# Row maxima of an attention kernel from 64-row products taken in pairs

## The chip, the cores and the metric

The kernel runs on one core of a Trainium2 chip. The metric is the device time of one execution in microseconds (us). Five engines of the core run their own instruction streams beside each other: TensorE (products; PE in the profile, its weight loads PEld), VectorE (DVE), ScalarE (ACT), GpSimd (POOL) and SyncE (SP, which issues DMA transfers). Products are written to PSUM, which has 8 banks of 128 x 512 float32 values.

## The reference

Two layers work on 1024 latent tokens (width 1024, a 16 x 64 grid) and 256 context tokens; the output is the latent stream after a last norm. Layer 0 has global attention (8 query heads, 2 key heads, all 1280 keys) beside banded attention (8 heads, 2 key heads, the 256 context keys and a band of 128 tokens to each side, with a learned sink logit per head). Layer 1 has a convolution branch beside attention over a 2-D neighbourhood (8 heads, 8 rows x 16 columns and the context keys, with a table of biases). Head width is 64.

```python
s = einsum("bqhgd,bkhd->bhgqk", q, k) * ATTN_SCALE      # 64 ** -0.5
s = s + bias                                            # band mask or bias table
p = softmax(concatenate([s, sink_col]))[..., :-1]       # sink in the banded heads only
out = einsum("bhgqk,bkhd->bqhgd", p, v)
```

All is float32. A softmax does not change when one number is subtracted from a whole row; the kernel subtracts the row's maximum, and a value near it does as well.

## The kernel before

**Numbers.** A float32 operand is held as two float32r values, a high part (the rounded value) and a low part (the rest), so that one accurate product becomes two or three fast ones. `split` (L323) makes both parts, the high one on ScalarE and the low one on GpSimd or VectorE. Projections are three products each (`mm3`, L346 to L349: high x high, high x low, low x high).

**Attention tiles.** Head width is 64 and the array has 128 rows, so a product of 128 rows holds two 64-row halves. For a group of 512 queries (four heads of 128 queries in layer 0, 512 queries of one head in layer 1):
- `QH`: the high part of Q in rows 0 to 63 and again in rows 64 to 127.
- `QL`: the low part of Q in rows 0 to 63, and above it in rows 64 to 67 minus the row maxima (rows 68 to 75 hold the two parts of the sink's term in the banded heads).
- `KA`: the high part of K in rows 0 to 63, its low part in rows 64 to 127.
- `KB`: the high part of K again in rows 0 to 63 (`copy_k`, L592, a ScalarE copy), ones in rows 64 to 67 (`k_tiles`, L381, for layer 1 and `kv_tiles`, L575, for layer 0).

A tile of scores is then two products into one bank: `KA` x `QH` (L503, 128 rows) and `KB` x `QL` (L507, 68 rows), the second of which subtracts the maxima too. ScalarE takes the exponential (L515), `split` makes both parts of the result, and `flush` (L435) multiplies with V in three products (L445 to L447, of which L446 has 64 output columns) that also sum the denominators. In the banded heads one further product per group (L450, 76 rows) adds the sink's part to the denominators.

**Row maxima.** They must be there before the first score tile of a group. `attn_prep` (L392) does this for a group: load Q, products of `QH` with `KA` into banks of the tag `mx` (`maxes`, L608 in layer 0, L1416 in layer 1), reductions on VectorE straight from the bank (L616, L627, L635, L1426, L1435), one small reduction over pieces, a transpose (L415), and a product with a mask (L416) that writes minus the maxima into `QL`. There are 40 groups in layer 0 (4 units of heads, each 10 query blocks, two of them with context keys alone) and 16 in layer 1. Per group there are:
- layer 0, all groups: four products of 256 context keys, two to a bank;
- layer 0, global heads, 8 of 10 blocks: eight products of 512 keys, one to a bank;
- layer 0, banded heads, 8 of 10 blocks: four products of 384 keys (256 at the ends);
- layer 1: four products of 256 keys, two to a bank, and four of 320 or 440 keys.

Every bank is filled and then reduced, and the tag `mx` has two banks, so that one can be filled while the other is reduced.

**Order of the work.** `attn_gen` (L428) yields after each step, and `weave` (L533) runs a fixed number of its steps against steps of a second generator with projection work (the next unit's projections, gates, output products). `prepare` (L473) runs a few steps of the preparations of groups further on in each step of the current group; a preparation is opened two groups ahead. This gives the program order. The order on each engine is then set by a planner that places instructions by its own estimate of when they are ready and by priorities (`later`, L294, moves the fill work back or forth by `FL`). Instructions on one engine run strictly in that order, so one that waits holds up all behind it.

`copy_k` runs in `last` (L640, L1412), that is, at the last tile of the last group but one of a unit or head, for the next one. It is followed by that group's own tail, and the first user of the copy is the first score tile of the next unit. SyncE issues the loads of Q (`load_q`), K and V (`load_kv`, `load_head`).

Of the kernel before, what the change touches and what calls it, by code (L numbers as in the profile page):

```python
# [18 lines left out]
P = 128  # L19
# [81 lines left out]
def tile_kernel(ctx: ExitStack, tc: tile.TileContext, a, out):  # L101
# [279 lines left out]
    def k_tiles(pool, n, bufs=1):  # L381
        KA = pool.tile([P, n * P], F32R, tag="KA", name=nm("KAt"), bufs=bufs)
        KB = pool.tile([P, n * P], F32R, tag="KB", name=nm("KBt"), bufs=bufs)
        GP.memset(KB[64:68, :].bitcast(F32), 1.0)
        Ks.append((KA, KB))

# [4 lines left out]

    def attn_prep(pool, g):  # L392
        QH = pool.tile([P, 512], F32R, tag="QH", name=nm("QH"), bufs=3)
        QL = pool.tile([P, 512], F32R, tag="QL", name=nm("QL"), bufs=3)
# [21 lines left out]
        VE.tensor_tensor(QL[64 : 64 + nr, :].rearrange("p (h q) -> p h q", h=4),  # L416
# [11 lines left out]
    def attn_gen(pool, groups, vshare, look, nexts=None):  # L428
# [6 lines left out]
        def flush():  # L435
# [12 lines left out]
            if last:  # L448
                if g.sink is not None:
                    PE.matmul(g.ov, g.skm(), g.QL[0:76, :], start=False, stop=True)  # L450
# [36 lines left out]
        for x, (g, t) in enumerate(items):  # L487
# [19 lines left out]
            PE.matmul(sf, KB[0:68, cs], cut(g.QL[0:68], q0, n), start=False, stop=True)  # L507
# [67 lines left out]
    def kv_tiles(u):  # L575

        if not both:
            for _ in range(2):
                both.append((a0.tile([P, NTOK], F32R, tag="KB", name=nm("KBt"), bufs=2),
                             a0.tile([P, 10, 192], F32R, tag="V", name=nm("Vt"), bufs=2)))  # L580
                GP.memset(both[-1][0][64:68, :].bitcast(F32), 1.0)
# [10 lines left out]
    def copy_k(KA, KB):  # L592
        SC.copy(KB[0:64, :], KA[0:64, :].bitcast(F32))

    def group0(u, qb):
        isb = u >= 2

        def load_q(QH, QL):
            src = Qd[u][qb].rearrange("(e d) s a t -> d s e (a t)", e=2)
            for dst, s in ((QH[0:64, :], 0), (QH[64:128, :], 0), (QL[0:64, :], 1)):  # L600
                SY.dma_start(dst.bitcast(F32).rearrange("d (e c) -> d e c", e=2), src[:, s])
# [6 lines left out]
        def maxes(QH, mp):  # L608
            KA = KAs[u]
            for i2 in range(2):  # L610
                mx = bank("mx", nm("mx"))
                for i in range(2):
                    hd = 2 * i2 + i
                    PE.matmul(mx[:, i * 256 : (i + 1) * 256], QH[:, hd * P : (hd + 1) * P], KA[:, 0:256],
                              start=True, stop=True)
                VE.tensor_reduce(mp[:, 2 * i2 : 2 * i2 + 2, 0], mx.rearrange("p (i k) -> p i k", i=2),  # L616
                                 axis=AX.X, op=ALU.max)
                yield
            if qb < 2:
                return  # L620
            for hd in range(4):
                q = QH[:, hd * P : (hd + 1) * P]
                if not isb:
                    for k in range(2):
                        mx = bank("mx", nm("mx"))
                        PE.matmul(mx, q, KA[:, 256 + k * 512 : 768 + k * 512], start=True, stop=True)  # L626
                        VE.tensor_reduce(mp[:, hd, 1 + k : 2 + k], mx, axis=AX.X, op=ALU.max)  # L627
                        yield
                else:
                    lo, hi = max(qb - 1, 2), min(qb + 2, 10)  # L630
                    n = (hi - lo) * P
                    mo = (lo - (qb - 1)) * P
                    mx = bank("mx", nm("mx"))
                    PE.matmul(mx[:, :n], q, KA[:, lo * P : hi * P], start=True, stop=True)
                    VE.tensor_tensor_reduce(out=mx[:, :n], in0=mx[:, :n], in1=bmask[:, mo : mo + n],  # L635
                                            op0=ALU.add, op1=ALU.max, accum_out=mp[:, hd, 1:2],
                                            scale=1.0, scalar=-3.0e38)
                    yield

        def last():  # L640
            if qb == QORD[-2] and u != ORDER[-1]:
                v = ORDER[ORDER.index(u) + 1]
                copy_k(KAs[v], KBs[v])
# [46 lines left out]
    with ExitStack() as p0x:  # L690
# [492 lines left out]
    with ExitStack():  # L1183
# [180 lines left out]
        tpool = ctx.enter_context(tc.tile_pool(name="t1", bufs=1, reuse_waits="tile"))  # L1364
        for _ in range(2):
# [10 lines left out]
        def group1(gi, hd, hf):  # L1376
# [35 lines left out]
            def last():  # L1412
                if hf == 0 and hd < 7:
                    copy_k(*heads[hd + 1])

            def maxes(QH, mp):  # L1416
                KA = Ks[hd % len(Ks)][0]
                for b in (1, 2, 0, 3):
                    if b in (1, 0):
                        mx = bank("mx", nm("mx1"))  # L1420
                        b0 = 1 - b
                        bb = (1, 2) if b else (0, 3)
                        for k in range(2):
                            PE.matmul(mx[:, k * 256 : (k + 1) * 256], QH[:, bb[k] * P : (bb[k] + 1) * P], KA[:, 0:256],
                                      start=True, stop=True)
                        VE.tensor_reduce(mp[:, bb[0] : bb[1] + 1 : bb[1] - bb[0], 0],  # L1426
                                         mx.rearrange("p (i k) -> p i k", i=2), axis=AX.X, op=ALU.max)
                        yield
# [3 lines left out]
                    PE.matmul(mx[:, :n].rearrange("p (t x) -> p t x", t=5), QH[:, b * P : (b + 1) * P],  # L1432
                              KA[:, o : o + 640].rearrange("p (t x) -> p t x", t=5)[:, :, r0 * 8 : r1 * 8],
# [369 lines left out]
```

## Time and profile before

| what | value |
|---|---|
| median of two timed runs | 1509.15 us (1508.86 to 1509.44) |
| the profiled execution: its own time, its span | 1508.76 us, 1506.7 us |
| granted TensorE clock, mean | 0.977 |
| TensorE busy, matmuls | 1424.8 us, 7006 |
| VectorE, GpSimd, ScalarE busy | 1086.2, 816.9, 750.3 us |
| layer 0 attention (with projections woven in) | about 120 to 920 us of the span |
| layer 1 attention | about 1160 to 1440 us |

How to read it: the span runs from the first to the last instruction, and the execution's own time has 2.1 us around it. A group of instructions is a line of the kernel, an engine, an operation, the names of the tiles, the shape (rows * columns of the array, then the output), how many there are, then the busy time, the mean duration of one and the idle time of the engine before them with what ended it. Products are pipelined: a duration includes the time through the array, so that durations overlap and the pace of products is the distance of their starts. In a timeline each row is a start, a length, an engine, a line and the instruction; neighbours of the same kind are merged into one row with a count.

### The profile page before, as it was taken

The page shows a single profiled execution, that of the slowest core. Times are in us where ns is not written, and L with a number is a line of the kernel's source. Part 1 is how long each engine was busy: PE and PEld are TensorE (multiplying, and loading weights), DVE is VectorE, ACT ScalarE, POOL GpSimd, SP SyncE. Part 2 cuts the span into 40 slices and gives each one's busy share as a digit, 9 for nine tenths or more (in the row PEclk, how much of TensorE's full clock was granted, in tenths as well). Part 3 has the DMA queues.
Part 4 walks back from the last instruction along what each step waited for, and adds up shares of the span by engine and source line. Part 5 has one row for each costly group of instructions (what it writes and reads, how often), then busy time and mean ns, then how long its engine had stood idle before and what let it go on. Part 6 is the DMA issues. An engine that isn't in the chain of part 4 may idle for free.

```text
span 1506.7 us, 22055 instructions
## 1 busy us (share of the span) xinstructions
PE 1424.8 (95%) x7006; PEld 1164.5 (77%) x7006; DVE 1086.2 (72%) x2139; ACT 750.3 (50%) x1536; POOL 816.9 (54%) x764
## 2 busy tenths in 40 slices
PE   7699999999999999999999989999999999999996
PEld 2598887987788678778888768888887878788775
DVE  5996787589957677555477676999938466677766
ACT  3541344446454765665455665443434354555563
POOL 3261463466555686776455765764543343364663
PEclk9799999999999999999999989999999999999998
DMA  9766245424541123641111122212596777797523
GB/s 351 261 201 190 73 123 179 144 67 122 161 133 47 45 84 119 218 156 45 49 42 43 60 77 80 86 65 69 160 315 197 209 219 209 231 292 219 189 63 119
DMA packets 182827, 215.23 MB, mean 143 GB/s; under 512 B 17196, under 2 KB 136184, under 8 KB 182712
## 3 DMA queue, kind: packets, MB, share of 16 engines
q1 hardware_dynamic: 176048, 202.26, 43.2%
q10 hardware_dynamic: 6664, 11.57, 2.4%
q8 instruction: 55, 0.90, 0.2%
q14 instruction: 60, 0.49, 0.1%
HBM read 151.64 MB, written 62.13 MB: 142 GB/s over the span
## 4 chain that ended last, share of the span: by engine, by line
PE 71%; DVE 13%; DMA 8%; issue 3%; POOL 2%; ACT 1%; SPq 1%; DVEq 0%; ACTq 0%; POOLq 0%
PE p L347 6%; PE p L348 6%; PE p L349 6%; PE ov L445 5%; PE ov L447 4%; PE ov L446 4%; PE po L347 4%; PE po L349 4%; PE po L348 4%; PE st L507 4%; PE st L503 4%; DMA mw<-in_mod_w_dram 3%; PE pg L347 2%; PE pq L349 2%; PE pq L347 2%
## 5 line engine op out<-in xcount | busy, mean ns | idle before, releaser
L328 POOL TENSOR_TENSOR pl<-pf,ph 128x512 fp32r<-128x512 f32 (+3 forms) x321 | 392.4, 1233 | 257.3 <-ACT ph L325 208.0
L328 POOL TENSOR_TENSOR wl<-wr,wh 128x256 fp32r<-128x256 f32 (+2 forms) x253 | 194.5, 787 | 160.5 <-ACT wh L325 112.4
L515 ACT ACTIVATE pf<-st 128x512 f32<-128x512 f32 x284 | 166.6, 596 | 179.6 <-PE st L507 129.9
L325 ACT CAST ph<-pf 128x512 fp32r<-128x512 f32 (+3 forms) x364 | 205.8, 578 | 24.0 <-PE ov L446 13.3
L347 PE MATMUL p<-hh,wh 128*128 128x512 f32 x448 | 177.6, 398 | 2.4 <-ACT wh L325 1.6
L348 PE MATMUL p<-hl,wh 128*128 128x512 f32 x448 | 178.0, 399 | 0.0
L349 PE MATMUL p<-hh,wl 128*128 128x512 f32 x448 | 173.1, 396 | 0.0
L325 ACT CAST wh<-wr 128x256 fp32r<-128x256 f32 (+2 forms) x260 | 101.6, 405 | 128.9 <-DMA wr<-in_od_d_dram 39.7
L445 PE MATMUL ov<-ph,Vt 128*128 128x512 f32 (+3 forms) x364 | 141.8, 390 | 10.1 <-DVE y L669 6.4
L503 PE MATMUL st<-QH,KAt 128*128 128x512 f32 (+3 forms) x364 | 139.7, 385 | 6.4 <-ACT pf L515 4.1
L447 PE MATMUL ov<-pl,Vt 128*128 128x512 f32 (+3 forms) x364 | 142.2, 392 | 3.7 <-DVE pl L328 1.9
L446 PE MATMUL ov<-ph,Vt 128*64 128x512 f32 (+3 forms) x364 | 139.5, 383 | 0.0
L507 PE MATMUL st<-QL,KBt 68*128 68x512 f32 (+3 forms) x364 | 135.6, 382 | 1.2 <-DVE QL L416 1.2
L1200 DVE SCALAR_TENSOR_TENSOR cps<-U,taps,cps 128x512 f32<-128x512 f32 x184 | 124.4, 749 | 0.1
L627 DVE TENSOR_REDUCE mp<-mx 128x1 f32<-128x512 f32 x128 | 85.6, 684 | 37.8 <-PE mx L626 37.1
L347 PEld LDWEIGHTS p<-hh,wh 128*128 128x128 f32 x448 | 84.5, 189 | 22.8 <-ACT wh L325 2.2
L349 PEld LDWEIGHTS p<-hh,wl 128*128 128x128 f32 x448 | 84.4, 188 | 20.1 <-issue 0.5
L348 PEld LDWEIGHTS p<-hl,wh 128*128 128x128 f32 x448 | 84.5, 189 | 19.0 <-issue 0.2
L447 PEld LDWEIGHTS ov<-pl,Vt 128*128 128x128 f32 x364 | 71.1, 195 | 27.6 <-POOL pl L328 5.1
L445 PEld LDWEIGHTS ov<-ph,Vt 128*128 128x128 f32 x364 | 71.4, 196 | 25.7 <-issue 6.1
L347 PE MATMUL pq<-wh,hh 128*128 128x384 f32 x256 | 88.0, 344 | 0.0
L349 PE MATMUL pq<-wh,hl 128*128 128x384 f32 x256 | 87.5, 342 | 0.0
(289 smaller groups left out, 3443.0 us busy)
## 6 DMA issues: line engine op xcount, KB each, us to landing
mw<-in_mod_w_dram SPq DMA_DIRECT2D x34, 512.0 KB, 5.9
Q<-qs SPq DMA_DIRECT2D x40, 256.0 KB, 2.6
QH<-Q SPq DMA_DIRECT2D x80, 128.0 KB, 2.8
bm<-in_d_bm_dram SPq DMA_DIRECT2D x16, 540.0 KB, 5.4
wr<-in_od_d_dram SPq DMA_DIRECT2D x64, 128.0 KB, 2.8
mw<-in_mod_w_dram SPq DMA_DIRECT2D x28, 256.0 KB, 3.0
wr<-in_ev_qkv_dram SPq DMA_DIRECT2D x32, 192.0 KB, 4.5
QD<-spq SPq DMA_DIRECT2D x48, 128.0 KB, 2.5
```

Of the source, the lines that this page charges most:

```text
L325: SC.copy(hi, src)
L328: (GP if leng == "g" else VE).tensor_tensor(lo, src, hi.bitcast(F32), op=ALU.subtract)
L347: PE.matmul(o, lh, rh, start=first, stop=False)
L348: PE.matmul(o, lh, rl, start=False, stop=False)
L349: done[0] = PE.matmul(o, ll, rh, start=False, stop=last)
L445: PE.matmul(o, V[:, 64:192], ph, start=(t == 0), stop=False)
L446: PE.matmul(cut(g.ov[0:64], q0, n), V[:, 0:64], ph, start=False, stop=False)
L447: pvs.append(PE.matmul(o, V[:, 64:192], pl, start=False, stop=(last and g.sink is None)))
L503: sts.append(PE.matmul(sf, KA[:, cs], cut(g.QH, q0, n), start=True, stop=False))
L507: PE.matmul(sf, KB[0:68, cs], cut(g.QL[0:68], q0, n), start=False, stop=True)
L515: SC.activation(pf[:, :n], st[:, :n], AF.Exp, scale=1.0 if g.bias else SCALE)
L1200: VE.scalar_tensor_tensor(pc, uc, w, pc, op0=ALU.mult, op1=ALU.add)
```

## The change

- The row maxima come from the high part of Q times the high part of K alone. Each product has 64 rows, and products go in pairs: one in rows 0 to 63 of the array (`QH` and `KA`, upper halves), one in rows 64 to 127 (`QH` and `KB`, lower halves), each into a bank of its own. Both are issued one behind the other, then the two reductions.
- For that `KB` holds the high part of K in rows 64 to 127. Ones move to rows 0 to 3, and rows 4 to 63 are zero. `QL` is turned over likewise: minus the maxima and the sink's terms in rows 0 to 11, the low part of Q in rows 64 to 127. Its three buffers are made once per layer and cleared (`clear_ql`), and then used in turn (`next_ql`).
- The second score product has 128 rows in place of 68, the sink's product 12 in place of 76.
- The copy of K moves from `last` to the front of the first `maxes` of a unit or head.
- In layer 0 heads are paired (0 with 2 and 1 with 3 for the context, 0 with 1 and 2 with 3 for the band), and in the global heads the two halves of the image keys. In layer 1 the context products of two query blocks go in the upper rows with an image product in the lower, twice, and then two image products together. The number of products, of their columns and of the reductions stays.

```diff
@@ -381,7 +381,8 @@
         KB = pool.tile([P, n * P], F32R, tag="KB", name=nm("KBt"), bufs=bufs)
-        GP.memset(KB[64:68, :].bitcast(F32), 1.0)
+        GP.memset(KB[0:64, :].bitcast(F32), 0.0)
+        GP.memset(KB[0:4, :].bitcast(F32), 1.0)
         Ks.append((KA, KB))
@@ -389,9 +390,20 @@
+    QLs = []
+
+    def next_ql():
+        QLs.append(QLs.pop(0))
+        return QLs[-1]
+
+    def clear_ql():
+        QLs[:] = [kvp.tile([P, 512], F32R, tag="QL", name=nm("QL"), bufs=3) for _ in range(3)]
+        for q in QLs:
+            GP.memset(q[0:64].bitcast(F32), 0.0)
+
     def attn_prep(pool, g):
         QH = pool.tile([P, 512], F32R, tag="QH", name=nm("QH"), bufs=3)
-        QL = pool.tile([P, 512], F32R, tag="QL", name=nm("QL"), bufs=3)
+        QL = next_ql()
         g.QH, g.QL = QH, QL
@@ -413,7 +425,7 @@
         PE.transpose(tr2[0:nr, 0:P], nmt[:, 0:nr].bitcast(F32), ident)
-        VE.tensor_tensor(QL[64 : 64 + nr, :].rearrange("p (h q) -> p h q", h=4),
+        VE.tensor_tensor(QL[0:nr, :].rearrange("p (h q) -> p h q", h=4),
                          tr2[0:nr, None, 0:P].broadcast_to([nr, 4, P]),
@@ -447,7 +459,7 @@
                 if g.sink is not None:
-                    PE.matmul(g.ov, g.skm(), g.QL[0:76, :], start=False, stop=True)
+                    PE.matmul(g.ov, g.skm(), g.QL[0:12, :], start=False, stop=True)
                 r1 = pool.tile([P, 8, 32], F32, tag="r1", name=nm("r1"), bufs=1)
@@ -504,7 +516,7 @@
                     PE.matmul(st[:, :n], lhs, rhs, start=False, stop=False)
-            PE.matmul(sf, KB[0:68, cs], cut(g.QL[0:68], q0, n), start=False, stop=True)
+            PE.matmul(sf, KB[:, cs], cut(g.QL, q0, n), start=False, stop=True)
             ph = pool.tile([P, 512], F32R, tag="ph", name=nm("ph"), bufs=look + 1)
@@ -578,7 +590,8 @@
                              a0.tile([P, 10, 192], F32R, tag="V", name=nm("Vt"), bufs=2)))
-                GP.memset(both[-1][0][64:68, :].bitcast(F32), 1.0)
+                GP.memset(both[-1][0][0:64, :].bitcast(F32), 0.0)
+                GP.memset(both[-1][0][0:4, :].bitcast(F32), 1.0)
                 GP.memset(both[-1][1][:, :, 128:192].bitcast(F32), 1.0)
@@ -590,14 +603,14 @@
     def copy_k(KA, KB):
-        SC.copy(KB[0:64, :], KA[0:64, :].bitcast(F32))
+        SC.copy(KB[64:128, :], KA[0:64, :].bitcast(F32))
             src = Qd[u][qb].rearrange("(e d) s a t -> d s e (a t)", e=2)
-            for dst, s in ((QH[0:64, :], 0), (QH[64:128, :], 0), (QL[0:64, :], 1)):
+            for dst, s in ((QH[0:64, :], 0), (QH[64:128, :], 0), (QL[64:128, :], 1)):
                 SY.dma_start(dst.bitcast(F32).rearrange("d (e c) -> d e c", e=2), src[:, s])
@@ -606,41 +619,51 @@
         def maxes(QH, mp):
...
+            KA, KB = KAs[u], KBs[u]
+            if qb == QORD[0] and u != ORDER[0]:
+                copy_k(KA, KB)
+
+            def two(qs, n, keys):
+                ms = [bank("mx", nm("mx")) for _ in range(2)]
+                for j in range(len(keys[0])):
+                    for s, K in enumerate((KA, KB)):
+                        r = slice(s * 64, s * 64 + 64)
+                        ks = keys[s][j]
+                        h_ = qs[s][j]
+                        PE.matmul(ms[s][:, j * n : (j + 1) * n], QH[r, h_ * P : (h_ + 1) * P], K[r, ks : ks + n],
+                                  start=True, stop=True)
+                return ms
+
+            ms = two(((0, 1), (2, 3)), 256, ((0, 0), (0, 0)))
+            for s, mx in enumerate(ms):
+                VE.tensor_reduce(mp[:, 2 * s : 2 * s + 2, 0], mx.rearrange("p (i k) -> p i k", i=2),
                                  axis=AX.X, op=ALU.max)
...
+            yield
+            yield
             if qb < 2:
                 return
...
+            if not isb:
+                for hd in range(4):
+                    ms = two(((hd,), (hd,)), 512, ((256,), (768,)))
+                    for k, mx in enumerate(ms):
                         VE.tensor_reduce(mp[:, hd, 1 + k : 2 + k], mx, axis=AX.X, op=ALU.max)
...
                     yield
+                    yield
+            else:
+                lo, hi = max(qb - 1, 2), min(qb + 2, 10)
+                n = (hi - lo) * P
+                mo = (lo - (qb - 1)) * P
+                for hd in (0, 2):
+                    ms = two(((hd,), (hd + 1,)), n, ((lo * P,), (lo * P,)))
+                    for k, mx in enumerate(ms):
+                        VE.tensor_tensor_reduce(out=mx[:, :n], in0=mx[:, :n], in1=bmask[:, mo : mo + n],
+                                                op0=ALU.add, op1=ALU.max, accum_out=mp[:, hd + k, 1:2],
+                                                scale=1.0, scalar=-3.0e38)
+                    yield
+                    yield
         def last():
...
+            pass
@@ -781,13 +804,13 @@
         bmt = a0.tile([P, 2, P], F32R, tag="bmt", name="bmt")
-        sk = a0.tile([76, P], F32R, tag="sk", name="sk")
+        sk = a0.tile([12, P], F32R, tag="sk", name="sk")
         cst = a0.tile([P, 512], F32, tag="ost", name="cst", bufs=2)
             SY.dma_start(cst[:, 0:256], a["k_bt"].rearrange("p a b -> p (a b)"))
-            SY.dma_start(cst[0:76, 256:384], a["k_sk"])
+            SY.dma_start(cst[0:12, 256:384], a["k_sk"])
         VE.tensor_copy(bmt, cst[:, 0:256].rearrange("p (a b) -> p a b", a=2))
-        VE.tensor_copy(sk, cst[0:76, 256:384])
+        VE.tensor_copy(sk, cst[0:12, 256:384])
@@ -959,10 +982,11 @@
         assert not tails
+        clear_ql()
         kv_tiles(ORDER[0])
             load_kv(ORDER[0], *PIECES[j])
-        SY.dma_start(KBs[ORDER[0]][0:64, :].bitcast(F32), Kd[ORDER[0]][0:64])
+        SY.dma_start(KBs[ORDER[0]][64:128, :].bitcast(F32), Kd[ORDER[0]][0:64])
         main = attn_gen(a0, [group0(u, qb) for u in ORDER for qb in QORD], VS0, LOOK0)
@@ -1362,6 +1386,7 @@
         tpool = ctx.enter_context(tc.tile_pool(name="t1", bufs=1, reuse_waits="tile"))
+        clear_ql()
         for _ in range(2):
@@ -1380,7 +1405,7 @@
                 SY.dma_start(QH.bitcast(F32), QD[i][e, 0:128, hf])
-                SY.dma_start(QL[0:64, :].bitcast(F32), QD[i][e, 128:192, hf])
+                SY.dma_start(QL[64:128, :].bitcast(F32), QD[i][e, 128:192, hf])
                 bm = tpool.tile([P, BMW], F32, tag="bm", name=nm("bm"), bufs=2)
@@ -1410,30 +1435,39 @@
             def last():
...
+                pass
             def maxes(QH, mp):
...
+                K = Ks[hd % len(Ks)]
+                if hf == 0 and hd:
+                    copy_k(*K)
+
+                def ctx(s, bb):
+                    r = slice(s * 64, s * 64 + 64)
+                    mx = bank("mx", nm("mx1"))
+                    for k in range(2):
+                        PE.matmul(mx[:, k * 256 : (k + 1) * 256], QH[r, bb[k] * P : (bb[k] + 1) * P], K[s][r, 0:256],
+                                  start=True, stop=True)
+                    return lambda: VE.tensor_reduce(mp[:, bb[0] : bb[1] + 1 : bb[1] - bb[0], 0],
+                                                    mx.rearrange("p (i k) -> p i k", i=2), axis=AX.X, op=ALU.max)
+
+                def img(s, b):
+                    r = slice(s * 64, s * 64 + 64)
                     r0, r1 = KROWS[b]
                     mx = bank("mx", nm("mx1"))
...
+                    PE.matmul(mx[:, :n].rearrange("p (t x) -> p t x", t=5), QH[r, b * P : (b + 1) * P],
+                              K[s][r, o : o + 640].rearrange("p (t x) -> p t x", t=5)[:, :, r0 * 8 : r1 * 8],
                               start=True, stop=True)
...
+                    return lambda: VE.tensor_tensor_reduce(out=mx[:, :n], in0=mx[:, :n], in1=bms[b], op0=ALU.add, op1=ALU.max,
+                                                           accum_out=mp[:, b, 1:2], scale=1.0, scalar=-3.0e38)
+
+                for a_, b_ in ((lambda: ctx(0, (1, 2)), lambda: img(1, 1)), (lambda: ctx(0, (0, 3)), lambda: img(1, 2)),
+                               (lambda: img(0, 0), lambda: img(1, 3))):
+                    x_, y_ = a_(), b_()
+                    x_()
+                    y_()
+                    yield
                     yield
@@ -1704,8 +1738,8 @@
     k["k_bd"] = (np.arange(12)[:, None] % 4 == np.arange(4)[None, :]).astype(f)
-    sk = np.zeros((76, 128), f)
-    sk[68:76, 64:] = 1
+    sk = np.zeros((12, 128), f)
+    sk[4:12, 64:] = 1
     k["k_sk"] = sk
```

More of the change, by code (lines that the diff above doesn't have):

```diff
@@ L608, in maxes @@
         def maxes(QH, mp):
[L609 to L616, printed above, removed]
+            KA, KB = KAs[u], KBs[u]
@@ L617, in maxes @@
+            ms = two(((0, 1), (2, 3)), 256, ((0, 0), (0, 0)))
+            for s, mx in enumerate(ms):
+                VE.tensor_reduce(mp[:, 2 * s : 2 * s + 2, 0], mx.rearrange("p (i k) -> p i k", i=2),
                                  axis=AX.X, op=ALU.max)
-                yield
+            yield
+            yield
             if qb < 2:
                 return
[L621 to L637, printed above, removed]
@@ L638, in maxes @@
                     yield
         def last():
-            if qb == QORD[-2] and u != ORDER[-1]:
-                v = ORDER[ORDER.index(u) + 1]
-                copy_k(KAs[v], KBs[v])
+            pass
         def mask(m):
@@ L1412, in last @@
             def last():
-                if hf == 0 and hd < 7:
-                    copy_k(*heads[hd + 1])
+                pass
             def maxes(QH, mp):
[L1417 to L1428, printed above, removed]
+                K = Ks[hd % len(Ks)]
[11 more added lines that the diff above has]
+                    r = slice(s * 64, s * 64 + 64)
                     r0, r1 = KROWS[b]
```

4 lines of the change are left out of this document (removed).

## The prediction

> **What bounds the kernel now.** I read the page first: span, busy shares, and the chain of work that ended last.
>
> ```profile
> span 1506.7 us, 22055 instructions
> PE 1424.8 (95%) x7006; PEld 1164.5 (77%) x7006; DVE 1086.2 (72%) x2139; ACT 750.3 (50%) x1536; POOL 816.9 (54%) x764
> PE 71%; DVE 13%; DMA 8%; issue 3%; POOL 2%; ACT 1%; SPq 1%; DVEq 0%; ACTq 0%; POOLq 0%
> ```
>
> TensorE is busy for 95% of the span and holds 71% of the chain; the next engine, VectorE, stands at 72% and 13%. The change touches the two stretches with attention in them, so I asked for the busy time of each engine there (columns: stretch, length, busy us of PE, PEld, DVE, ACT, POOL, clock, DMA share, GB/s).
>
> ```profile
> 120.00:480.00 360.00, 349.41 (x1837) 300.89 (x1837) 274.19 (x589) 160.27 (x356) 183.23 (x152) 1.00 0.41 124
> 480.00:920.00 440.00, 423.75 (x1976) 332.67 (x1975) 288.97 (x501) 254.13 (x473) 284.07 (x240) 0.98 0.27 84
> 1160.00:1440.00 280.00, 265.71 (x1359) 222.60 (x1358) 193.35 (x477) 143.27 (x318) 126.05 (x144) 0.98 0.71 217
> ```
>
> In these 1080 us TensorE is busy for 349.4 + 423.8 + 265.7 = 1038.9 us, 96%. It has 41 us of waits there, so what the change gives or takes on TensorE reaches the end nearly whole.
>
> **What the touched products cost.** The groups by line and shape:
>
> ```profile
> L626 PE MATMUL mx<-KAt,QH 128*128 128x512 f32 x128 | 49.8, 404 | 1.9 <-DVE mp L627 1.7
> L614 PE MATMUL mx<-KAt,QH 128*128 128x256 f32 x160 | 30.7, 289 | 3.4 <-DMA QH<-Q 2.7 <-DVE mp L635 0.6
> L634 PE MATMUL mx<-KAt,QH 128*128 128x384 f32 x48 | 16.3, 350 | 1.3 <-DVE mp L635 0.7 <-DVE mp L616 0.6
> L634 PE MATMUL mx<-KAt,QH 128*128 128x256 f32 x16 | 4.6, 285 | 0.0
> L1424 PE MATMUL mx<-KAt,QH 128*128 128x256 f32 x64 | 13.6, 295 | 5.9 <-DMA QH<-QD 5.8
> L1432 PE MATMUL mx<-KAt,QH 128*128 128x440 f32 x32 | 11.7, 370 | 0.0
> L1432 PE MATMUL mx<-KAt,QH 128*128 128x320 f32 x32 | 9.7, 320 | 0.0
> L450 PE MATMUL ov<-QL,sk 76*128 76x512 f32 x20 | 8.0, 398 | 0.0
> ```
>
> The mean durations (404 ns for 512 columns) are no price, because products overlap. The price is the time from start to start, which the timeline gives (columns: start, length, instruction, count):
>
> ```profile
> 496.32 0.40 PE L445 MATMUL ov<-ph,Vt 128*128 128x512 f32 x1
> 496.55 0.39 PE L446 MATMUL ov<-ph,Vt 128*64 128x512 f32 x1
> 496.78 0.62 PE L626 MATMUL mx<-KAt,QH 128*128 128x512 f32 x2
> 497.24 0.40 PE L447 MATMUL ov<-pl,Vt 128*128 128x512 f32 x1
> ...
> 831.46 0.43 PEld L614 LDWEIGHTS mx<-KAt,QH 128*128 128x128 f32 x2
> 831.70 0.40 PE L614 MATMUL mx<-KAt,QH 128*128 128x256 f32 x2
> 831.94 0.40 PE L445 MATMUL ov<-ph,Vt 128*128 128x512 f32 x1
> ```
>
> Two row-maximum products of 512 columns take 497.24 - 496.78 = 0.46, so 0.232 us each; two of 256 take 0.24, so 0.118 each. Between them I go by columns: 0.147 for 320, 0.174 for 384, 0.200 for 440. The weight load of a product starts with the product before it (831.46 against 831.70), so it is hidden. All row maxima together: 128 x 0.232 + (160 + 16 + 64) x 0.118 + 48 x 0.174 + 32 x 0.200 + 32 x 0.147 = 77.5 us. That is the whole stake. Perfect pairing would leave, pair by pair, 64 x 0.232 + 32 x 0.161 (the mean of 384 and 256 columns as they occur) + 40 x 0.236 + 32 x 0.236 + 16 x 0.147 = 39.4, a gain of 38 us or 2.5% of 1508.8.
>
> **What a switch of the array's shape costs.** The new products use 64 rows; everything around them uses 128. The trace has no 64-row product, but it has a 2-row one (L204) in a stream of 128-row ones, and a 2-column one (L197).
>
> ```profile
> 39.84 0.34 PE L349 MATMUL pq<-wh,hc 128*128 128x384 f32 x1
> 40.01 0.34 PE L347 MATMUL pq<-wh,hc 128*128 128x384 f32 x1
> 40.36 0.34 PE L349 MATMUL pq<-wh,hc 128*128 128x384 f32 x1
> 40.63 0.32 PEld L204 LDWEIGHTS trm<-ident,mrow 2*128 2x128 f32 x4 [0.25 <-issue]
> 40.63 0.41 PE L204 MATMUL trm<-ident,mrow 2*128 2x2 f32 x4
> ...
> 36.09 0.08 PEld L197 LDWEIGHTS pm<-mw,csil 128*2 128x2 f32 x1 [0.34 <-issue]
> 36.52 0.09 PEld L197 LDWEIGHTS pm<-mw,csil 128*2 128x2 f32 x1 [0.34 <-issue]
> 35.66 1.88 PE L197 MATMUL pm<-mw,csil 128*2 128x512 f32 x4
> 37.47 0.19 PEld L349 LDWEIGHTS pq<-wh,hc 128*128 128x128 f32 x1 [0.86 <-issue]
> 37.57 0.19 PEld L347 LDWEIGHTS pq<-wh,hc 128*128 128x128 f32 x1
> 37.47 0.44 PE L349 MATMUL pq<-wh,hc 128*128 128x384 f32 x1
> 37.75 0.34 PE L347 MATMUL pq<-wh,hc 128*128 128x384 f32 x1
> ```
>
> Going in: the last 384-column product starts at 40.36 and streams until 40.53. The weight load of the 2-row product, which ought to have started at 40.36, starts at 40.63: it was held until 0.09 us after the array had run dry. Coming out: four L197 products at 0.43 from 35.66 end at 37.38; the next weight load starts 0.09 later, at 37.47, and the product behind it is followed only at 37.75, 0.28 on instead of 0.174, because its load of about 0.106 lay bare. So a switch is 0.093 of drain plus 0.106 of exposed load, 0.20 us, each way. Against this stands L446 above: 128 rows by 64 columns, 364 times between full products, at an unbroken pace of 0.23. Not every smaller shape drains, and that is the main doubt. I side with L204, since it is the one row that is smaller in rows, as the new products are.
>
> The Trainium skill ("TensorEngine Tiling (Array Packing)", Tiling Modes, Key Properties) says that changing the tiling mode drains the array. By that rule L446 would drain 728 times at 0.093, 68 us, which the trace does not show; L204 and L197 do show it. The Trainium skill ("PSUM — Partial Sum Buffer", PSUM: the matmul accumulator) notes that float32r products force the column mask to the full array, which would fit both.
>
> **Part by part, on TensorE.** A pair between full products costs: 0.093 drain, 0.106 for the first weight load, something for the second load, one product's stream, and 0.200 to go back. The second load is hidden at best (0) and queued behind the first at worst (0.107, the distance of the loads at 37.47 and 37.57; the four 2-row loads take at most 0.32/4 = 0.08 each); I take 0.05.
> - Layer 0 global heads, 64 pairs of 512: 0.093 + 0.106 + 0.05 + 0.232 + 0.200 = 0.681 against 0.464, +0.217: +13.9 us.
> - Layer 0 banded heads, 32 pairs: stream 0.161, so 0.610 against 0.322: +9.2.
> - Layer 0 context, 40 sets of four 256s: stream 0.236, so 0.685 against 0.472: +8.5.
> - Layer 1, 32 sets of two 256s in the upper rows and one 440 in the lower. Products start in order, so the 440 starts with the second 256 (0.118 + 0.200), and its load is hidden: 0.717 against 0.436: +9.0.
> - Layer 1, 16 pairs of 320: 0.596 against 0.294: +4.8.
> - The sink product L450 goes from 76 rows to 12, so it becomes a product smaller in rows too: 0.093 + 0.106 + 0.232 + 0.200 = 0.631 against 0.235, 20 times: +7.9.
>
> Together +53 us on TensorE. Lower bound, with a first load at the 0.08 of the 2-row rows, the second hidden and the 440 wholly overlapped: 38 us. Upper bound, where switches drain and the two halves do not run together at all (38 us more): 91. Of the 53 I take 80% to the end, 43 us: within a stretch that is 96% busy the other engines catch up while TensorE drains, and some of its 41 us of waits go.
>
> The score product L507 goes from 68 rows to 128. L450 with 76 rows lasts 398 ns, L626 with 128 lasts 404, so the height has no price: nothing.
>
> **The other engines.**
>
> ```profile
> L593 ACT CAST KBt<-KAt 64x1536 fp32r<-64x1536 f32 (+1 forms) x11 | 15.6, 1414 | 17.4 <-DMA KAt<-KD 14.2 <-DMA KAt<-K 3.2
> L384 POOL MEMSET KBt<- 4x1536 f32 x2 | 2.7, 1374 | 0.1
> L581 POOL MEMSET KBt<- 4x1280 f32 x2 | 2.3, 1162 | 19.6 <-DVE macc L247 17.3 <-DVE mrun L247 2.3
> L627 DVE TENSOR_REDUCE mp<-mx 128x1 f32<-128x512 f32 x128 | 85.6, 684 | 37.8 <-PE mx L626 37.1
> ```
>
> The copy of K moves from the end of the last group but one to the front of the next unit's first maxima, 10 times. It now stands in ScalarE's queue ahead of exponentials, and the lower product of the first pair waits for it with everything behind it on TensorE: 0 to 1.41 us each, 0 to 14 us; I take 2, since the order is planned with other work put between. GpSimd gets four more clears of K tiles (2 x 1.37 + 2 x 1.16) and six of QL, a 512-column clear being at most 0.5 by those rows: 8 us on an engine at 54%, all at the fronts of the attention stretches; 0 to 5, I take 1. A pair fills both row-maximum banks at once, and the next pair needs both reductions (2 x 0.684) done; before, banks alternated and TensorE waited 1.7 us in all for L627. Pairs lie two steps of the weave apart, as two single products did: 0 to 10, I take 1. VectorE's own work is unchanged.
>
> Sum: 43 + 2 + 1 + 1 = 47 us over the profiled execution's 1508.8 (its span of 1506.7 and 2.1 around it; the median of the runs is 1509.15, 0.4 more): **1555 us**.
>
> **Rivals.**
> 1. Pairs without a drain, faster. If 64-row products enter as L446 does, TensorE gives back between 25 us (weight loads at 0.107 in series, which then bound the sets of four at 0.43) and 38 (streams alone). At 80 to 90% that is 20 to 34: 1475 to 1489, likeliest 1481. For it: L446's unbroken pace. Against: L204. The Trainium skill ("TensorE: Matmul & The Clock Gate", Part 3) gives a pack one product's time plus about 4 ns per further tile; by that a pair would be 0.236, near the end of this rival, but it speaks of packs alone and not of the products around them.
> 2. No change. Either the hardware runs the 64-row float32r products as full ones, unpaired and undrained, as it seems to do with L446's columns; then only the 4 us of the other engines are left, 1513. Or it drains but the loads stay hidden: a 512 pair is 0.418 against 0.464, a set of four 0.422 against 0.472, the layer 1 sets lose 0.07, the sink 0.19, in sum +2 us, 1515. With either and the stalls at their bounds: 1500 to 1530.
> 3. Slower still: drains, and the halves in series, 91 x 0.8 + 4, 1586. The deciding point is whether both halves' products start together.
>
> **Chances.** Forecast with rival 3: 0.55, times from 1508.8 + 38 x 0.75 = 1537 to 1586. Rival 2: 0.23. Rival 1: 0.22. About 2% (30 us) is what a measurement of this kernel can tell from no change. Of the forecast's 0.55 nearly 0.06 stays under 30 us, so slower 0.49; of rival 1 a third is over 30 us, so faster 0.07; the rest, 0.44, is within. The range must take in rival 2 and most of rival 1, and leave out the ends: 1482 to 1577; the forecast's own range is 1537 to 1577.
>
> **What would show it.** Right: in the timeline, the weight load of the first 64-row product starts about 0.09 after the stream before it ends, and the first full product after a pair carries about 0.1 more; pairs of 512 take 0.6 to 0.75 from the last full product's end to the next one's real start; TensorE's share rises or stays while the span grows by some 45 us, all of it in the attention stretches and none between 920 and 1120. Wrong: the loads of both halves start behind the product before them as all loads do now, both halves start together, and the product after them follows at 0.24 from the pair's start (rival 1), or at 0.46 with no gaps (rival 2). A growth of the waits of TensorE for the K copy or for the reductions, by over 10 us, would put the cause elsewhere.

## The result and the profile after

The changed kernel takes **1633.66 us** (median of two runs, 1633.09 to 1634.24) against 1509.15, a ratio of **1.0825** (95% interval 1.0779 to 1.0872): 124.5 us slower. The forecast was 1555 with a range up to 1577, so the sign was right and the size 2.7 times too small.

The page of the changed kernel, the same parts as before:

```profile
span 1631.3 us, 22042 instructions
PE 1554.7 (95%) x7006; PEld 1156.2 (71%) x7006; DVE 1082.3 (66%) x2139; ACT 755.6 (46%) x1536; POOL 819.9 (50%) x774
PE 78%; DMA 8%; DVE 6%; issue 3%; POOL 2%; ACT 2%; SPq 1%; DVEq 0%; POOLq 0%; ACTq 0%
```

TensorE is busy 130 us longer with the same 7006 products and holds 78% of the chain instead of 71%. The other engines change little: VectorE is busy 4 us less, ScalarE 5 and GpSimd 3 us more. The loss lies where the change is: the convolution between the two attention stretches has the same busy times before (first row) and after (second row; columns as in the prediction).

```profile
937.00:1092.00 155.00, 154.18 (x689) 124.97 (x687) 145.00 (x227) 68.36 (x120) 94.05 (x85) 1.00 0.34 97
```

```profile
1035.00:1190.00 155.00, 154.02 (x689) 124.86 (x687) 144.92 (x227) 68.24 (x120) 93.88 (x85) 1.00 0.33 97
```

It only begins 98 us later: that much is lost in layer 0, and the rest in layer 1.

The waits of TensorE that the prediction had named as signs of another cause stay small. For the copy of K they are 4.5 us (columns: who waited for whom, us in total, times, the longest), and for the reductions of the row maxima 3.4 us in all:

```profile
PE mx L633 <- ACT KBt L606: 4.0, 1, 4.0
PE mx L633 <- DVE mp L649: 2.1, 4, 0.9
PE mx L1459 <- ACT KBt L606: 0.5, 1, 0.5
```

The granted clock of TensorE differs too: 0.970 in both runs of the changed kernel, 0.977 in the profiled run before. Two stretches with attention show it (the eighth column is the clock; the prediction's rows for 480 to 920 and 1160 to 1440 have 0.98):

```profile
520.00:1010.00 490.00, 472.91 (x1947) 324.85 (x1947) 287.20 (x494) 252.52 (x466) 285.38 (x243) 0.96 0.24 75
1240.00:1540.00 300.00, 289.72 (x1348) 218.24 (x1347) 188.62 (x452) 144.40 (x315) 119.00 (x138) 0.97 0.68 207
```

Around 695 us of the span, where the granted clock is 0.50, full products of 512 columns start 0.43 us apart (694.29, 694.72, 695.14) in place of 0.232. If all of the clock that was not granted were time lost, it would be 0.030 x 1633.66 = 49 us against 0.023 x 1509.15 = 35: up to 14 us of the 124.5, by this estimate. Why less was granted no run here shows.

The timeline of the changed kernel shows one pair of 512 columns in a global head (L633 is the row-maximum product; PEld rows are weight loads):

```profile
484.22 0.34 PE L348 MATMUL pq<-wl,hh 128*128 128x384 f32 x1
484.48 0.18 PEld L633 LDWEIGHTS mx<-KAt,QH 64*128 64x128 f32 x1 [0.25 <-DVE r L469]
484.48 0.50 PE L633 MATMUL mx<-KAt,QH 64*128 64x512 f32 x1
484.91 0.19 PEld L349 LDWEIGHTS pq<-wh,hl 128*128 128x128 f32 x1 [0.25 <-issue]
484.91 0.44 PE L349 MATMUL pq<-wh,hl 128*128 128x384 f32 x1
485.19 0.34 PE L347 MATMUL pq<-wh,hh 128*128 128x384 f32 x1
...
486.17 0.18 PEld L633 LDWEIGHTS mx<-KBt,QH 64*128 64x128 f32 x1 [0.26 <-issue]
486.17 0.49 PE L633 MATMUL mx<-KBt,QH 64*128 64x512 f32 x1
486.59 0.19 PEld L349 LDWEIGHTS pq<-wh,hl 128*128 128x128 f32 x1 [0.24 <-issue]
486.59 0.44 PE L349 MATMUL pq<-wh,hl 128*128 128x384 f32 x1
```

Two things are to be seen. First, the switch of the array's height is there and has the forecast price: the product at 484.22 streams until 484.39, the weight load comes 0.09 later at 484.48; the 64-row stream ends near 484.82 and the next load starts at 484.91; and the full product at 484.91 is followed at 485.19, 0.28 on instead of 0.174. From 484.39 to the real start of the next full product (485.19 - 0.174 = 485.02) are 0.63 us. Second, **the pair is no pair.** The lower half runs 1.7 us later, with projection products between, and pays the whole switch again.

Counted over the trace, a visit being an unbroken run of products on 12 or 64 rows, TensorE makes **355 visits** for the 500 such products, where the forecast had 204. Of the 64 pairs of 512 columns only six are a visit of just their two halves. This is one (products first, then weight loads):

```profile
561.30 0.39 PE L519 MATMUL st<-QL,KBt 128*128 128x512 f32 x1
561.62 0.50 PE L633 MATMUL mx<-KAt,QH 64*128 64x512 f32 x1
561.62 0.49 PE L633 MATMUL mx<-KBt,QH 64*128 64x512 f32 x1
562.05 0.50 PE L459 MATMUL ov<-pl,Vt 128*128 128x512 f32 x1
562.39 0.39 PE L515 MATMUL st<-QH,KAt 128*128 128x512 f32 x1
...
561.62 0.18 PEld L633 LDWEIGHTS mx<-KAt,QH 64*128 64x128 f32 x1 [0.35 <-issue]
561.62 0.18 PEld L633 LDWEIGHTS mx<-KBt,QH 64*128 64x128 f32 x1
```

Both loads start together and both products too. From the end of the stream before (561.30 + 0.232 = 561.53) to the real start of the next full product (562.39 - 0.232 = 562.16) are 0.63 us, as long as for a single product. So the two halves do run side by side, wholly; it was hardly used.

The account on TensorE: a visit of one 512 takes 0.624 (median of 104 without another wait), of one 256 0.508, of two 256s on one half 0.629, of one 384 0.569, of a sink 0.627. Less the streams that is 0.390 to 0.395 in each; I take 0.392. 355 x 0.392 = 139 us, less some 4 us of streams that did run beside each other, is 135 us added; 124.5 arrived at the end.

### The profile page after: what moved, and what is told of

It is laid out like the page before. It is cut to its first block, busy times and chain, and to the rows that moved or that the text cites. A ratio compares the mean times of both kernels' runs of the same rounds, so it can differ in the third digit from the quotient of the medians.

```text
span 1631.3 us, 22042 instructions
## 1 busy us (share of the span) xinstructions
PE 1554.7 (95%) x7006; PEld 1156.2 (71%) x7006; DVE 1082.3 (66%) x2139; ACT 755.6 (46%) x1536; POOL 819.9 (50%) x774
## 4 chain that ended last, share of the span: by engine, by line
PE 78%; DMA 8%; DVE 6%; issue 3%; POOL 2%; ACT 2%; SPq 1%; DVEq 0%; POOLq 0%; ACTq 0%
PE p L347 6%; PE p L348 6%; PE p L349 6%; PE mx L633 6%; PE st L515 5%; PE ov L457 5%; PE ov L459 5%; PE ov L458 4%; PE st L519 4%; PE po L347 4%; PE po L348 4%; PE po L349 4%; PE pq L348 3%; PE pq L349 3%; PE pq L347 3%
## 5 line engine op out<-in xcount | busy, mean ns | idle before, releaser
L515 PE MATMUL st<-QH,KAt 128*128 128x512 f32 (+3 forms) x364 | 149.8, 413 | 5.4 <-ACT pf L527 3.3
L457 PE MATMUL ov<-ph,Vt 128*128 128x512 f32 (+3 forms) x364 | 146.0, 401 | 7.8 <-DVE y L692 3.6
L459 PE MATMUL ov<-pl,Vt 128*128 128x512 f32 (+3 forms) x364 | 145.5, 401 | 3.9 <-POOL pl L328 1.9
L519 PE MATMUL st<-QL,KBt 128*128 128x512 f32 (+3 forms) x364 | 137.3, 386 | 0.9 <-DVE QL L428 0.8
L515 PEld LDWEIGHTS st<-QH,KAt 128*128 128x128 f32 x364 | 69.7, 192 | 36.9 <-issue 9.8
L348 PE MATMUL pq<-wl,hh 128*128 128x384 f32 x256 | 89.9, 351 | 0.0
```

The costliest lines, as they stand in the source:

```text
L348: PE.matmul(o, lh, rl, start=False, stop=False)
L457: PE.matmul(o, V[:, 64:192], ph, start=(t == 0), stop=False)
L459: pvs.append(PE.matmul(o, V[:, 64:192], pl, start=False, stop=(last and g.sink is None)))
L515: sts.append(PE.matmul(sf, KA[:, cs], cut(g.QH, q0, n), start=True, stop=False))
L519: PE.matmul(sf, KB[:, cs], cut(g.QL, q0, n), start=False, stop=True)
```

## The experiments

The theory after the traces: the price is per visit, 0.39 us, whatever is done in it; the count was wrong, because the planner splits pairs. Rivals: the halves cost something by themselves; or the rest of the change (moved copy, clears, both banks filled at once) carries a good part. Ratios are against runs of the kernel before on the same chip.

**Full height back** (`e1_full_rows`): only the row-maximum products change.

```diff
-  PE.matmul(ms[s][...], QH[r, ...], K[r, ks : ks + n], ...)
+  PE.matmul(ms[s][...], QH[:, ...], KA[:, ks : ks + n], ...)
```

> The changed kernel with only the row maxima put back to full height (128 rows, high part of Q against high and low part of K, one product behind the other as the planner likes); the new layout of KB and QL, the clears, the moved copy of K and the 12-row sink product stay. Theory (visits): what costs is each visit of TensorE to a lower height, 0.40 us beside the streams, and the planner, which put other products between the two of a pair, made 355 of them out of the 204 I had counted. Here 20 visits are left (the sinks): 1509 + 20 x 0.40 = 1517, with up to 5 us for copy and clears 1515 to 1522. Rival (the rest of the change: copy of K in ScalarE's queue, clears, both banks filled at once): a good part of the 124 us stays, over 1540.

Measured: 1525.11 us, ratio 1.0098 (1.0076 to 1.0120). That is above the 1515 to 1522 expected and under the rival's 1540. So 108 of the 124 us go with the height of the row maxima (and with it the wait for the copy of K, since products of `KA` alone do not read it). The 16 us that stay are twice what the sinks' visits explain. A sink in this run (its 12 rows are one visit):

```profile
174.11 0.39 PE L459 MATMUL ov<-pl,Vt 128*128 128x512 f32 x1
174.43 0.50 PE L462 MATMUL ov<-QL,sk 12*128 12x512 f32 x1
174.86 0.74 PE L519 MATMUL st<-QL,KBt 128*128 128x512 f32 x2
```

**Pairs held together** (`e2_pairs_adjacent`): both products of a pair wait for the reduction that frees the later of the two banks, the reductions keep their order, and the products get a higher priority in the planned order.

```diff
+  with later(-300):
       m = PE.matmul(ms[s][...], QH[r, ...], K[r, ks : ks + n], ...)
+  tc.add_manual_dep(m.ins, last_reduction_of_the_pair_before.ins.name, ...)
...
+  with tc.issue_after(first_reduction_of_the_pair.ins):
       VE.tensor_reduce(...)
```

> The changed kernel with the two products of a pair held together: both wait for the reduction that frees the second bank, and they get a higher priority, so that the planner puts them side by side. In the planned order 223 visits to a lower height are left of 355. Visits theory: 1509 + 223 x 0.40 = 1598, less 36 us of streams that now run beside each other, 1562 (1552 to 1575). Rival (the two halves run in series even side by side): 1598 or more. Rival (rest of the change): about 1634 as before.

Measured: 1556.21 us, ratio 1.0315 (1.0287 to 1.0344), near the 1562 expected. The three edits together save 77 us.

**The same on one half** (`e3_adjacent_one_half`):

```diff
-  K, r = (KA, KB)[s], slice(s * 64, s * 64 + 64)
+  K, r = KA, slice(0, 64)
```

> As the run with adjacent pairs, but both products of a pair use rows 0 to 63 (high part of Q, upper half of KA), so that they can't run beside each other. 203 visits in the planned order. Visits theory: streams as in the kernel before, so 1509 + 203 x 0.40 = 1590 (1582 to 1600), though it has 20 visits fewer than the run with adjacent pairs; the difference between the two, with 8 us for those visits, is what running side by side is worth, about 36 us. Rival (halves in series anyway): this one is faster than the other by 8 us.

Measured: 1564.14 us, ratio 1.0366 (1.0348 to 1.0384). The time is well under the 1590 expected, and only 8 us over the run before. The timeline of this run, two 512s in one visit:

```profile
471.74 0.39 PE L515 MATMUL st<-QH,KAt 128*128 128x512 f32 x1
472.06 0.73 PE L646 MATMUL mx<-KAt,QH 64*128 64x512 f32 x2
472.72 0.49 PE L519 MATMUL st<-QL,KBt 128*128 128x512 f32 x1
473.05 0.39 PE L458 MATMUL ov<-ph,Vt 128*64 128x512 f32 x1
```

From 471.97 to 472.82 are 0.85 us, one stream (0.23) more than for a pair on both halves. So the halves do run side by side, and the theory holds on TensorE: its visits add some 79 us here (203 visits, no stream saved), 56 in the run with pairs on both halves. At the end 55 and 47 us arrive, 70% and 84%. What TensorE lost came through at different shares, and I had taken it whole; that was the miss of this expectation. The granted clock may be what parts the shares: its mean is 0.976 over the runs of this kernel, 0.972 with pairs on both halves and 0.979 before, which as lost time is up to 5 and 11 us; without them 50 of 79 and 36 of 56 arrive, 63% and 64%. This is an estimate, and no run tested it.

**The kernel before on 64 rows** (`e4_before_64rows`):

```diff
-  PE.matmul(mx[...], QH[:, ...], KA[:, ...], ...)
+  PE.matmul(mx[...], QH[0:64, ...], KA[0:64, ...], ...)
```

> The kernel before with one edit: each row-maximum product takes rows 0 to 63 alone (high part of Q, high part of K); no pairs, no new layout, no moved copy. 310 visits in the planned order. Visits theory: 1509 + 310 x 0.40 = 1633, that is nearly the whole loss of the change from the height alone (1615 to 1640). Rival (the rest of the change costs): well below, 1509 to 1560.

Measured: 1605.13 us, ratio 1.0634 (1.0614 to 1.0654). No pairs, no new layout, and 96 us lost for 310 visits, which add 310 x 0.392 = 122 us on TensorE (79% arrive). That is under the expected 1615, since again not all of it arrives, and far above the rival's 1560. The planner also orders this kernel's products differently from the kernel before; the run with priority alone, below, shows that another order can cost some 10 us by itself.

**The sink at full height as well** (`e5_full_rows_sink`): the table `sk` is filled up with zero rows, and the product takes all of `QL`.

```diff
-  PE.matmul(g.ov, g.skm(), g.QL[0:12, :], ...)
+  PE.matmul(g.ov, g.skm(), g.QL, ...)
```

> The run with full-height maxima (1525 us, 16 over before), with the sink's product taken over all 128 rows too (the rows of its table above 11 are zero). No product smaller in rows is left in the attention. Visits theory: its trace gives a 12-row sink 0.627 against 0.235 of its stream, so 20 x 0.39 = 8 us less: 1517. The other 8 us of the 16 stay; they belong to the rest of the change. Rival (the sinks are hidden, all 16 are of the rest): 1525.

Measured: 1521.69 us, ratio 1.0095 (1.0074 to 1.0117). Against 1.0098 without this edit that is 0.0003 less, with about 0.003 either way, so the 8 us that I expected (0.0053) are not there whole; a part of them, at the 70% seen above some 5 or 6 us, lies at the edge of what these runs can tell. The profiled spans differ by 6.3 us (1525.6 and 1519.3), but the first is of the longest of its four runs. Left open.

**The copy of K back in its place** (`e6_full_rows_sink_copy_back`): the copy leaves `maxes` and returns to `last`.

```diff
-  if qb == QORD[0] and u != ORDER[0]: copy_k(KA, KB)     # in maxes
+  if qb == QORD[-2] and u != ORDER[-1]: copy_k(KAs[v], KBs[v])     # in last
```

> The same, with the copy of K back at the last tile of the last group but one. If the moved copy carries the rest of the 16 us: 1509 to 1511. If the rest lies in the new layout, the clears or the planner's other order: it stays where the run without this edit is, near 1517.

Measured: 1522.37 us, ratio 1.0092 (1.0074 to 1.0110). With row maxima at full height the place of the copy costs nothing that can be seen. This does not test it in the changed kernel: here the row maxima read `KA` alone and never wait for the copy, while there the lower products read `KB`, and TensorE waits 4.5 us for it (rows above).

**Priority alone** (`e7_before_priority`):

```diff
+  with later(-300):
       PE.matmul(mx[...], QH[:, ...], KA[:, ...], ...)
```

> The kernel before with nothing but a higher priority for the row-maximum products in the planned order, as the runs with adjacent pairs have it. Theory: priority has no part in their result, so this stays within 0.5% of before, 1504 to 1516. Rival (the higher priority by itself saves time, and hid a part of the visits' price in the runs with adjacent pairs, which cost 0.27 us per visit at the end against 0.39 on TensorE): 1490 to 1500, and then it beats both kernels.

Measured: 1517.86 us, ratio 1.0061 (1.0040 to 1.0082): just over the 1516 expected and slower, not faster, so there is no sign that the priority hid a part of the price in the two runs above. It also shows that the order matters by itself: an edit that touches no instruction costs 0.6% by another order.

**Pairs held together without the priority** (`e8_pairs_adjacent_no_priority`): the wait for the later bank and the kept order of the two reductions.

```diff
   m = PE.matmul(ms[s][...], QH[r, ...], K[r, ks : ks + n], ...)
+  tc.add_manual_dep(m.ins, last_reduction_of_the_pair_before.ins.name, ...)
...
+  with tc.issue_after(first_reduction_of_the_pair.ins):
       VE.tensor_reduce(...)
```

> The run with adjacent pairs without the higher priority: only the wait of both products of a pair for the reduction that frees the second bank. 226 visits in the planned order against 223 with the priority and 355 without either. Theory: the pairs were split because their two banks come free at different times, so this one edit brings nearly all back: 1552 to 1562, as with the priority (1556). Rival (priority does it): clearly above, toward 1600.

Measured: 1546.85 us, ratio 1.0258 (1.0241 to 1.0275), 87 us under the changed kernel and a little under the 1552 expected, with 226 visits. The 9 us under the run with the priority go with a higher granted clock (mean 0.979 against 0.972), so they are no price of the priority that these runs show. A pair in its timeline:

```profile
467.95 0.39 PE L515 MATMUL st<-QH,KAt 128*128 128x512 f32 x1
468.27 0.50 PE L646 MATMUL mx<-KAt,QH 64*128 64x512 f32 x1
468.28 0.49 PE L646 MATMUL mx<-KBt,QH 64*128 64x512 f32 x1
468.70 0.50 PE L519 MATMUL st<-QL,KBt 128*128 128x512 f32 x1
469.04 0.40 PE L458 MATMUL ov<-ph,Vt 128*64 128x512 f32 x1
```

So the pairs were split because their two banks come free one after the other: without the wait the planner issues the upper product when its bank is free, fills in others, and issues the lower one when the second reduction is done. (The order of the reductions was not fixed without the wait, so what it does alone is not known.)

**The new layout alone** (`e9_layout_alone`): layout, clears, and 128-row score and sink products, with the loops of the row maxima and the place of the copy as in the kernel before.

```diff
-  ms = two(((hd,), (hd,)), 512, ((256,), (768,)))
-  for k, mx in enumerate(ms):
+  for k in range(2):
+      mx = bank("mx", nm("mx"))
+      PE.matmul(mx, QH[:, ...], KA[:, 256 + k * 512 : 768 + k * 512], ...)
...
-  PE.matmul(g.ov, g.skm(), g.QL[0:12, :], ...)
+  PE.matmul(g.ov, g.skm(), g.QL, ...)
```

> The new layout alone (KB and QL turned over, clears, buffers of QL in turn, second score product and sink over 128 rows), with the row maxima as in the kernel before: full height, one product, its reduction, a yield. The same with two products and then two reductions between yields took 14 us over before (0.92%). If that order of issue is their cause (both banks filled, then both reduced): 1506 to 1511 here. If the layout or the clears are: 1517 to 1523.

Measured: 1516.26 us, ratio 1.0062 (1.0039 to 1.0085), between the two expectations. Of the 0.95% that the run with full height and full sink loses, the layout may carry two thirds and the order of issue the rest, but the intervals touch; it was not settled. In the run with full height and full sink most of it is waiting of TensorE, not work:

```profile
span 1519.3 us, 22023 instructions
PE 1427.7 (94%) x7006; PEld 1160.9 (76%) x7006; DVE 1075.0 (71%) x2139; ACT 750.8 (49%) x1536; POOL 821.9 (54%) x774
```

It is idle for 1519.3 - 1427.7 = 91.6 us, against 1506.7 - 1424.8 = 81.9 before.

**The kernel before on 96 rows** (`e10_before_96rows`):

```diff
-  PE.matmul(mx[...], QH[:, ...], KA[:, ...], ...)
+  PE.matmul(mx[...], QH[0:96, ...], KA[0:96, ...], ...)
```

> The kernel before with row-maximum products over rows 0 to 95 in place of 0 to 63 (the high part of Q against the high part of K and half of the rows of its low part). With 64 rows this edit took 96 us. Theory: the array has a height of 32, 64 or 128, 96 rows still use the full one, no visit, no cost: 1505 to 1515, as the 68-row score products of the kernel before cost nothing. Rival (any height under 128 drains, or the missing rows cost something): 1590 or more.

Measured: 1511.56 us, ratio 1.0021 (1.0004 to 1.0037). TensorE has the same planned order as in the kernel before. The groups of the 512-column products, first with 96 rows, then with 64:

```profile
L626 PE MATMUL mx<-KAt,QH 96*128 96x512 f32 x128 | 49.6, 404 | 1.8 <-DVE mp L627 1.7
```

```profile
L626 PE MATMUL mx<-KAt,QH 64*128 64x512 f32 x128 | 61.2, 496 | 1.3 <-DVE mp L627 1.0
```

With 96 rows the mean is the 404 ns of full height; with 64 it is 92 more, the exposed load of the product itself. So rows left out cost nothing by themselves: 96 rows go as 128 do, and so do the 68 and 76 rows of the kernel before (L507 and L450, with starts 0.236 and 0.235 us apart for 512 columns). The price comes with 64 rows; between 64 and 68 no run has a product.

**The best form of the change** (`e11_pairs_adjacent_sink`): the pairs held together by the wait, and the sink at full height.

```diff
+  tc.add_manual_dep(m.ins, last_reduction_of_the_pair_before.ins.name, ...)
...
-  PE.matmul(g.ov, g.skm(), g.QL[0:12, :], ...)
+  PE.matmul(g.ov, g.skm(), g.QL, ...)
```

> The run with adjacent pairs without the priority (1547), with the sink over 128 rows: 208 visits in the planned order against 226, 18 x 0.39 = 7 us less on TensorE, so 1539 to 1545. That is the best form of the change that I have; the theory says that no pair can win: a pair of 512 columns costs 0.626 in its visit and 0.464 outside. Rival (it could): at or under 1509.

Measured: 1543.99 us, ratio 1.0232 (1.0210 to 1.0255). It lies within the 1539 to 1545 expected and does not reach the kernel before.

## Why the prediction was wrong

- **What bounds the kernel**: right. TensorE lost 135 us by the count of visits, and 124.5 arrived, 92% where I had taken 80%. But the 124.5 hold more than the visits: some 8 to 14 us go with the rest of the change, and up to 14 with the lower granted clock, which the prediction did not have. Without both some 97 to 103 us are left, 72 to 76%; that is an estimate, since no run parts the three.
- **The switch, 0.093 + 0.106 each way**: right. The load of the first 64-row product was held for 0.09 us, the product behind it carried 0.11, and a visit costs 0.392 beside its stream. That L446 (fewer columns) does not drain and the 64-row products do is as weighed. The reason given for going by L204 was too wide, though: it was not the one row smaller in rows, for L507 with 68 rows and L450 with 76 ran among full products without a drain.
- **The price of a pair, 0.681**: a little high. It is 0.63 where a pair stays together, because the two loads start together (0 in place of my 0.05). Rival 3, halves in series, falls with it.
- **The step that failed: "pairs lie two steps of the weave apart", and with it the count of 204 visits.** I took the order in which the program issues a pair for the order in which TensorE gets it. I had named the very cause (a pair fills both banks, the next needs both reductions) and costed it as a wait of TensorE, 0 to 10 us, 1 taken. TensorE did not wait: the planner filled the time between the two banks with full-height products, and each half became a visit of its own. That is 355 visits in place of 204, 151 x 0.392 = 59 us, and 32 of the 36 us that the side by side was to give back. From 53 us: 53 + 59 + 32 - 8 for the second loads = 136, the 135 found.
- As a check on the rest: the runs in which pairs stay together, 223 and 226 visits, take 1556 and 1547 us, about what I forecast for the change. On TensorE the terms were good, and the count was not. That the total fits as well is partly luck: less than 80% of the visits' time arrives, and the rest of the change and the clock add more than the 4 us I had for the other engines.
- **The other engines**: the moved copy makes TensorE wait 4.5 us in the changed kernel (2 taken); what of it reaches the end no run shows. The rest of the layout and its order of issue, 8 to 14 us where I had 2; the causes in it were not told apart.
- **Rivals 1 and 2** (no drain, or undrained and unpaired) fall: the rows at 484.48 and 484.91 show both drains, and the 0.28 from 484.91 to 485.19 shows the load laid bare that the second form of rival 2 had hidden.

## What to carry to other kernels

Products on 64 rows or fewer did not come cheap among full ones: here every change of height and back cost 0.39 us, so a visit must save more than that (over 860 columns of stream at 0.232 us for 512) to pay, and a pair of 512 saves 0.232. Where two instructions are only worth something side by side, look at what makes each of them ready; if that differs, a planner that places each instruction when it is ready parts them, and a wait of both on the later event puts them together (87 us here, with the order of the reductions kept). And count such visits in the planned order of the engine, not in the program's.

## What was not expected of the hardware

- Two 64-row products on different halves of the array run wholly beside each other, loads included: both loads at 561.62, both products at 561.62, and 0.63 us for the pair as for a single one.
- The price does not depend on what is changed to: 12 rows (0.627 with 512 columns) cost what 64 do (0.624), while 96 rows (ratio 1.0021, the mean of a product unchanged at 404 ns), 76 and 68 carry none of it.
